# A diffusion-transformer layer: fillers gathered ahead of the first conditioning sums, fewer between them, and the second group's sums one product later

## The chip, the cores and the metric

The kernel runs on one core of a Trainium2 chip. The metric is the device time of one execution in microseconds (us). A core has TensorE (PE; PEld is its weight load), VectorE (DVE), ScalarE (ACT), GpSimd (POOL) and SyncE (SP, which here only issues DMAs). Each works through its own queue of instructions in order.

## The reference

One layer on 256 latent tokens and 256 context tokens of width 2048, in f32. A conditioning vector `c` (and `c_ctx` for the context) makes shifts, scales and gates; the modulated tokens go through one projection for queries, keys and values; windowed and global attention, an output projection, and a SwiGLU network follow.

```python
def ada_mods(cond, w_ada, b_ada):
    m = jnp.einsum('bd,de->be', jax.nn.silu(cond), w_ada) + b_ada      # (2048) x (2048, 12288)
    return [t[:, None, :] for t in jnp.split(m, 6, axis=-1)]
...
sh1, sc1, g1, sh2, sc2, g2 = ada_mods(c, w_ada[layer], b_ada[layer])
csh1, csc1, ... = ada_mods(c_ctx[None, :], w_ada[layer], b_ada[layer])
qa, ka, va, qb, kb, vb = mixer_qkv(x * (1 + sc1) + sh1, w_in[layer], ...)      # u @ w_in, heads, norms
qac, kac, vac, ... = mixer_qkv(ctx * (1 + csc1) + csh1, w_in[layer], ...)
x = layer_norm(ALPHA * x + g1 * (attention(...) @ w_out[layer]), ...)
x = layer_norm(ALPHA * x + g2 * swiglu(x * (1 + sc2) + sh2, ...), ...)
```

The weights are 281 MB; the first thing needed of them are the columns of `w_ada` that give shift and scale of the first 128 channels.

## The kernel before

**Precision.** Each f32 product is made of three matmuls (lines 292 to 294): both operands are split into a high part (a ScalarE cast, `hi`, `uh`) and the rest (a VectorE subtraction, `lo`, `ul`), and hi x hi, lo x hi and hi x lo are summed in PSUM. "A product" below is such a triple, on a bank `acc` of 128 x 512.

**Groups.** The 2048 channels enter the first projection in five groups of 1, 1, 2, 4 and 8 blocks of 128 (`GROUPS`), so that work can start when the shifts and scales of the first block are there. Group 0 has 16 products (six column blocks of `w_in`; two or four row tiles each), and so has group 1.

**Lead-in.** TensorE first runs fillers: `warm(wps, n)` issues n matmuls of the identity with itself (line 342), whose results nobody reads. It then turns `c` and `c_ctx`, which came as rows (`crow`), into columns by one matmul (line 348); ScalarE applies silu (`cs`). The shifts and scales of a group are sums over 2048 rows of `w_ada`: `flow_columns` loads 1 MB for the shifts and 1 MB for the scales and multiplies by `cs` (line 594, 32 output rows at a time, four side by side). For the first group the loads are cut in quarters of 256 KB (line 514), and `quarters` sums a quarter at a time, with fillers after the first three quarters of each MB. Between the two MB the flips (transposes) of the first block of x and ctx (`xt`, `cxt`, line 698) and of the bias (line 368) are pulled in. After the last sums: two fillers, a ScalarE copy `ada` (line 628), small sums with `sel` (line 633), two VectorE additions to shift and scale, seven more fillers, and the first product.

**Order.** A planner (`Flow`) lists all steps of the first part with an estimated duration and sets the order of each engine's queue by simulating them. `F.pulls` overrides it: a pair (trigger, steps) takes the steps out of their place and emits them right behind the trigger. `lead[P, ...]` are the steps of the second group (P = 128 is its first channel): `"both"` its sums over 2 MB, `"copy"`, `"sums"` and `"adds"` what follows on them, `flip`, `mod` and `rest` the transposes of x and ctx, the modulation and the low part. `made` is the list of products of group 0, and `(made, PULL)` stands for its entry PULL, counted from 0. The planner also has 56 filler steps of one matmul each; those whose number is in `WARMS` are emitted, the others are empty.

**Buffers.** Loads of weights go to six buffers of 1 MB (`raw`, `araw`), besides small loads of group 0. SP issues them in order; an issue waits until its buffer has been read, for the conditioning weights by the sums of line 594.

Of the kernel before, what the change touches and what calls it, by code (L numbers as in the profile page):

```python
# [22 lines left out]
P = 128  # L23
# [21 lines left out]
NB4 = 18  # L45
T2K = 5
WARM = 56
WARMS = (32, 33, 35, 36, 37, 38, 39, 40, 41)
SLACK = 2500
AHEAD = 14  # L50
EARLY_G = 2
# [2 lines left out]
LAG_S = 2  # L54
PUT, GET, PLACE = 6, 8, 9
TAIL = 3
PULL = 11
SEED_G = 4
LANDING = 4500, 2500

# [157 lines left out]
def dit_layer(ctx: ExitStack, tc: tile.TileContext, x, c, cx, c_ctx, w_ada, b_ada, w_in, q_norm_g,  # L218
# [15 lines left out]
    def wk_bank():  # L234
        return wk_ps.tile([P, NB], F32, tag="wk", name="wk")
# [104 lines left out]
    def warm(wps, n):  # L340
        for _ in range(n):
            nc.tensor.matmul(wps, lhsT=ident, rhs=ident, start=True, stop=True)  # L342

    wps = Buf("wk")
    wps.t = wk_bank()[:, :P]
    warm(wps.t, 5)
    cps = wk_bank()
    nc.tensor.transpose(cps[:, : 2 * KD], crow, ident[: 2 * KD, : 2 * KD])
    cs = main.tile([P, 72 * 4], F32, tag="cs", name="cs")
# [3 lines left out]
        cps[:, : 2 * KD].rearrange("p (s k) -> p s k", s=2),  # L353
        AF.Silu,
    )


    sel = main.tile([P, 4], F32, tag="sel", name="sel")
# [100 lines left out]
    def const_tables():  # L459
        nc.gpsimd.tensor_scalar_mul(nsink, sinkb, -1.0)  # L460
        for t in range(NT):
            for g, cg, sg in ((gq, cosQ, sinQ), (gk, cosK, sinK)):
# [18 lines left out]
    F = Flow({"raw": RAW_BUFS, "araw": ADA_BUFS, "hl": HL_BUFS, "acc": 4, "wk": 4, "b4": NB4, "t2k": T2K},  # L481
             {"SP": 2100.0, "PE": 3800.0, "ACT": 4300.0, "DVE": 4000.0, "POOL": 4000.0})
# [6 lines left out]
    def t2k(name, shape=(P, NB), dtype=F32):  # L489
        return pa.tile(list(shape), dtype, tag="t2k", name=name, bufs=T2K)  # L490
# [11 lines left out]
    def flow_load(w, k0, nk, c0, width, where=("raw", "araw"), cut=1, small=False):  # L502
        room = Buf(*where)

        def fn():
            if small:
                room.t = b4([P, 2 * NB], F32, "raw1")[:, : nk * width]
                nc.sync.dma_start(room.t, w[k0 * P : (k0 + 1) * P, c0 : c0 + width])
                return
            if cut > 1:  # L510
                room.t = pools[room.pool].tile([P, G4 * NB], F32, tag="raw", name="raw")
                for q in range(0, nk, nk // cut):
                    n = nk // cut
                    nc.sync.dma_start(
                        room.t[:, q * width : (q + n) * width].rearrange("p (k n) -> p k n", k=n),
                        w[(k0 + q) * P : (k0 + q + n) * P, c0 : c0 + width].rearrange("(k p) n -> p k n", p=P),
                    )
                return
            room.t = pools[room.pool].tile([P, G4 * NB], F32, tag="raw", name="raw")[:, : nk * width]
            nc.sync.dma_start(  # L520
                room.t.rearrange("p (k n) -> p k n", k=nk),
                w[k0 * P : (k0 + nk) * P, c0 : c0 + width].rearrange("(k p) n -> p k n", p=P),
            )

        return room, F.add("SP", dma_ns(nk * width * P * 4, width * 4), fn, take=[room])
# [52 lines left out]
    last_load, lead = [], {}  # L578

    def flow_columns(c0, ncol, shift, scale, ats, at):  # L580

        width = ncol * P
        n1 = ncol == 1
        nk = G4 * NB // width
        ns = KD // nk
        bank, prev = Buf("wk"), None

        def fn(g, i, raw, k0, k1):
            if g == i == k0 == 0:
                bank.t = wk_bank()  # L590
            for c in range(k0, k1):
                k = g * nk + c
                j = k % 4
                nc.tensor.matmul(  # L594
                    bank.t[32 * j : 32 * j + 32, :width], lhsT=cs[:, 4 * k + 2 - 2 * i : 4 * k + 34 - 2 * i],
                    rhs=raw.t[:, c * width : (c + 1) * width],
                    start=(i == 0 and k < 4), stop=(i == 1 and k >= KD - 4),
                )

        for g in range(ns):  # L600
            F.at = ats[g]
            (r0, l0), (r1, l1) = (flow_load(w_ada, g * nk, nk, c0 + i * D, width, cut=1 if c0 else 4) for i in range(2))
            last_load[:] = [l1]
            ns1 = nk / 4 * (40 + 1.67 * width)
            if c0:
                def both(g=g, r0=r0, r1=r1):
                    fn(g, 0, r0, 0, nk)
                    fn(g, 1, r1, 0, nk)

                prev = F.add("PE", 2 * ns1 + 420, both, [l0, l1, prev], [bank] if g == 0 else [], [r0, r1])  # L610
            else:
                def quarters(i, r):
                    for q in range(4):
                        fn(0, i, r, 4 * q, 4 * q + 4)
                        if q < 3:
                            warm(wps.t, 1 + i)

                prev = F.add("PE", ns1, lambda r=r0: quarters(0, r), [l0, prev], [bank] if g == 0 else [], [r0])
                lead["sum"] = prev
                prev = F.add("PE", ns1, lambda r=r1: quarters(1, r), [l1, prev], [], [r1])  # L620
            if g == 0:
                lead[c0, "both"] = prev
        F.at = at
        sb, ps = Buf("t2k"), Buf("wk")

        def copy():
            sb.t = t2k("ada")
            nc.scalar.copy(sb.t[:, :width], bank.t[:, :width])

        def sums():  # L630
            ps.t = wk_bank()
            for j in range(ncol):
                nc.tensor.matmul(ps.t[:, 4 * j : 4 * j + 4], lhsT=sb.t[:, j * P : (j + 1) * P], rhs=sel, start=True, stop=True)

        def add(i):
            pv = ps.t[:, 0 : 4 * ncol].rearrange("p (j i s) -> p j i s", i=2, s=2)
            bs, bc = (bcol[:, k : k + ncol, None].to_broadcast([P, ncol, 2]) for k in (c0 // P, c0 // P + KD))
            if i == 0:
                nc.vector.tensor_tensor(shift, pv[:, :, 0, :], bs, op=ALU.add)
            else:  # L640
                nc.vector.scalar_tensor_tensor(scale, pv[:, :, 1, :], 1.0, bc, op0=ALU.add, op1=ALU.add)

        a = F.add("ACT", 60 + 0.9 * width, copy, [prev], [sb], [bank])
        b = F.add("PE", 224 * ncol, sums, [a], [ps], [sb])
        adds = [F.add("DVE", 160, lambda i=i: add(i), [b], give=[ps]) for i in range(2)]
        if n1:
            lead[c0, "copy"], lead[c0, "sums"], lead[c0, "adds"] = a, b, adds
        return a, adds
# [586 lines left out]
    def warm_step(i):  # L1235
        if i in WARMS:
            warm(wps.t, 1)
# [175 lines left out]
    made = lead["products", 0]  # L1413
    F.pulls.append(((lead["products", 1], 3), [lead[2 * P, "both"]]))
    F.pulls.append(((made, PULL), [lead[P, "both"]]))
    F.pulls.append(((made, PULL + 1), [lead[P, "copy"]]))
    F.pulls.append(((made, PULL + 2), [lead[P, "sums"], *lead[P, "adds"], flip0, flip1]))
    F.pulls.append(((made, PULL + 3), [mod0, rest0, mod1, rest1]))
    zroom = [Buf("wk"), Buf("wk")]
    for i in range(2):  # L1420
        F.add("PE", 210, lambda i=i: z_flip(0, 2 * i), [a], [zroom[i]])
# [361 lines left out]
```

## Time and profile before

| | |
|---|---|
| median of 3 runs | 1137.32 us (1136.08 to 1137.8) |
| profiled execution | 1140.03 us, span of its instructions 1138.2 us |
| TensorE busy | 1117.6 us (98%), matmul records 5265 |
| VectorE / ScalarE / GpSimd busy | 842.2 / 548.0 / 40.0 us |
| DMA | 321.26 MB, mean 282 GB/s |
| first product starts | 17.95 us into the span |

Times in the views count from the span's start. A row of the timeline groups equal instructions that follow on each other; "x8" counts records. What stands in brackets is idle time of that engine ahead of the row and who ended it. Matmuls overlap: a row's duration reaches beyond the start of the next, so the pace is read from start to start.

### The profile page before, as it was taken

The page shows a single profiled execution, that of the slowest core. Times are in us where ns is not written, and L with a number is a line of the kernel's source. Part 1 is how long each engine was busy: PE and PEld are TensorE (multiplying, and loading weights), DVE is VectorE, ACT ScalarE, POOL GpSimd, SP SyncE. Part 2 cuts the span into 40 slices and gives each one's busy share as a digit, 9 for nine tenths or more (in the row PEclk, how much of TensorE's full clock was granted, in tenths as well). Part 3 has the DMA queues.
Part 4 walks back from the last instruction along what each step waited for, and adds up shares of the span by engine and source line. Part 5 has one row for each costly group of instructions (what it writes and reads, how often), then busy time and mean ns, then how long its engine had stood idle before and what let it go on. Part 6 is the DMA issues. An engine that isn't in the chain of part 4 may idle for free.

```text
span 1138.2 us, 14088 instructions
## 1 busy us (share of the span) xinstructions
PE 1117.6 (98%) x5265; PEld 896.3 (79%) x5265; DVE 842.2 (74%) x1066; ACT 548.0 (48%) x790; POOL 40.0 (4%) x82
## 2 busy tenths in 40 slices
PE   8999999999999999999999999999999999999996
PEld 6666678788887787888888888888888888888884
DVE  4754579899989988787767566766766788676576
ACT  2322454777874455545464444454544334333342
POOL 1000050110100001000000000000000000000000
PEclk9999999999999999999999999999999999999998
DMA  9999999776999689999867777777687988887541
GB/s 307 324 381 392 389 372 371 271 220 222 360 326 397 212 311 345 324 317 309 321 214 241 228 238 237 219 245 255 216 266 240 313 313 319 315 290 252 194 148 74
DMA packets 178317, 321.26 MB, mean 282 GB/s; under 512 B 8732, under 2 KB 43196, under 8 KB 175943
## 3 DMA queue, kind: packets, MB, share of 16 engines
q1 hardware_dynamic: 177528, 320.03, 81.0%
q8 instruction: 41, 0.67, 0.2%
q10 hardware_dynamic: 720, 0.33, 0.1%
q14 instruction: 28, 0.23, 0.1%
HBM read 304.07 MB, written 16.25 MB: 281 GB/s over the span
## 4 chain that ended last, share of the span: by engine, by line
PE 89%; DVE 4%; DMA 3%; ACT 2%; issue 1%; POOL 0%; SPq 0%; DVEq 0%; ACTq 0%; POOLq 0%
PE acc L292 27%; PE acc L294 27%; PE acc L293 27%; PE wk L594 2%; PE wk L1024 2%; DMA raw<-in_w_in_dram 1%; DMA pd<-hx 1%; DVE lo L545 1%; DVE lo L283 1%; DVE adav L415 1%; DMA raw<-in_w_up_dram 1%; PE wk L292 1%; PE wk L294 1%; PE wk L293 1%; PE wk L342 1%
## 5 line engine op out<-in xcount | busy, mean ns | idle before, releaser
L283 DVE TENSOR_TENSOR lo<-raw,hi 128x1024 fp32r<-128x1024 f32 x258 | 311.8, 1221 | 172.1 <-ACT hi L282 167.6
L282 ACT CAST hi<-raw 128x1024 fp32r<-128x1024 f32 x258 | 270.7, 1055 | 333.7 <-PE acc L294 288.3
L293 PE MATMUL acc<-lo,u2h 128*128 128x512 f32 x704 | 274.0, 389 | 0.8 <-DVE lo L283 0.8
L292 PE MATMUL acc<-hi,u2h 128*128 128x512 f32 x704 | 274.7, 390 | 0.0
L294 PE MATMUL acc<-hi,u2l 128*128 128x512 f32 x704 | 274.1, 389 | 0.0
L293 PEld LDWEIGHTS acc<-lo,u2h 128*128 128x128 f32 x704 | 132.2, 188 | 28.5 <-DVE lo L283 1.1
L292 PEld LDWEIGHTS acc<-hi,u2h 128*128 128x128 f32 x704 | 132.1, 188 | 28.2 <-ACT u2h L1558 0.8
L294 PEld LDWEIGHTS acc<-hi,u2l 128*128 128x128 f32 x704 | 132.1, 188 | 27.8 <-DVE u2l L1559 0.5
L542 ACT CAST hi<-raw 128x1024 fp32r<-128x1024 f32 (+1 forms) x86 | 87.7, 1031 | 108.3 <-DMA raw<-in_w_in_dram 51.5
L292 PE MATMUL acc<-hi,hTh 128*128 128x512 f32 x344 | 135.6, 394 | 0.4 <-ACT acc L1708 0.4
L294 PE MATMUL acc<-hi,hTl 128*128 128x512 f32 x344 | 133.9, 389 | 0.0
L293 PE MATMUL acc<-lo,hTh 128*128 128x512 f32 x344 | 133.9, 389 | 0.0
L415 DVE SCALAR_TENSOR_TENSOR adav<-raw,cs,adav 128x512 f32<-128x512 f32 (+1 forms) x128 | 121.3, 947 | 11.6 <-DMA raw<-in_w_ada_dram 9.4
L545 DVE TENSOR_TENSOR lo<-raw,hi 128x1024 fp32r<-128x1024 f32 (+1 forms) x86 | 101.7, 1193 | 19.0 <-ACT hi L542 18.8
L292 PE MATMUL acc<-hi,uh 128*128 128x512 f32 x256 | 103.0, 402 | 2.4 <-DVE kvacc L781 1.0
L293 PE MATMUL acc<-lo,uh 128*128 128x512 f32 x256 | 100.2, 391 | 1.7 <-DVE lo L545 1.7
L294 PE MATMUL acc<-hi,ul 128*128 128x512 f32 x256 | 100.1, 391 | 0.0
L292 PEld LDWEIGHTS acc<-hi,hTh 128*128 128x128 f32 x344 | 64.6, 188 | 15.1 <-issue 1.0
L293 PEld LDWEIGHTS acc<-lo,hTh 128*128 128x128 f32 x344 | 64.6, 188 | 14.1 <-issue 1.0
L294 PEld LDWEIGHTS acc<-hi,hTl 128*128 128x128 f32 x344 | 64.6, 188 | 13.5
L292 PEld LDWEIGHTS acc<-hi,uh 128*128 128x128 f32 x256 | 48.1, 188 | 20.1 <-issue 6.4
L293 PEld LDWEIGHTS acc<-lo,uh 128*128 128x128 f32 x256 | 48.1, 188 | 11.8 <-DVE lo L545 2.7
(219 smaller groups left out, 1148.8 us busy)
## 6 DMA issues: line engine op xcount, KB each, us to landing
raw<-in_w_ada_dram SPq DMA_DIRECT2D x70, 1024.0 KB, 7.6
raw<-in_w_gate_dram SPq DMA_DIRECT2D x44, 1024.0 KB, 5.3
raw<-in_w_up_dram SPq DMA_DIRECT2D x44, 1024.0 KB, 5.2
raw<-in_w_down_dram SPq DMA_DIRECT2D x44, 1024.0 KB, 4.9
raw<-in_w_ada_dram SPq DMA_DIRECT2D x48, 512.0 KB, 5.5
raw<-in_w_in_dram SPq DMA_DIRECT2D x18, 1024.0 KB, 6.9
raw<-in_w_out_dram SPq DMA_DIRECT2D x16, 1024.0 KB, 8.5
pd<-hx SPq DMA_DIRECT2D x64, 128.0 KB, 4.0
```

Of the source, the lines that this page charges most:

```text
L282: nc.scalar.copy(hi[:, :n], raw[:, s : s + n])
L283: nc.vector.tensor_tensor(lo[:, :n], raw[:, s : s + n], hi[:, :n].bitcast(F32), op=ALU.subtract)
L292: nc.tensor.matmul(ps, lhsT=xh, rhs=w[0], start=first, stop=False, skip_group_check=seeded)
L293: nc.tensor.matmul(ps, lhsT=xh, rhs=w[1], start=False, stop=False, skip_group_check=seeded)
L294: nc.tensor.matmul(ps, lhsT=xl, rhs=w[0], start=False, stop=last, skip_group_check=seeded)
L342: nc.tensor.matmul(wps, lhsT=ident, rhs=ident, start=True, stop=True)
L415: nc.vector.scalar_tensor_tensor(a[:, c : c + piece], raw[:, f : f + piece], cs[:, 4 * (g * (G4 * NB // w) + j) + 2, None], a[:, c : c + p ...
L542: nc.scalar.copy(hl.hi[:, :n], raw.t[:, s : s + n])
L545: nc.vector.tensor_tensor(hl.lo[:, :n], raw.t[:, s : s + n], hl.hi[:, :n].bitcast(F32), op=ALU.subtract)
L594: nc.tensor.matmul(bank.t[32 * j : 32 * j + 32, :width], lhsT=cs[:, 4 * k + 2 - 2 * i : 4 * k + 34 - 2 * i], rhs=raw.t[:, c * width : (c + ...
L1024: nc.tensor.matmul(o_ps.t[:, : 2 * P].rearrange("p (g q) -> p g q", q=32), lhsT=v, rhs=pv[:, k], start=k == 0, stop=k == 3)
```

## The change

Three places. The fillers ahead of the first sums become twelve, seven before the flip of `c` and five after it; those within the first MB go, and within the second there is one each after its second and third quarter (two each after the first three, before). Of the planner's fillers six are emitted instead of nine. And `PULL` goes from 11 to 12, with the pulled steps of the second group regrouped.

```diff
-WARMS = (32, 33, 35, 36, 37, 38, 39, 40, 41)
+WARMS = (32, 33, 35, 36, 37, 38)
...
-PULL = 11
+PULL = 12
...
-    warm(wps.t, 5)
+    warm(wps.t, 7)
     cps = wk_bank()
     nc.tensor.transpose(cps[:, : 2 * KD], crow, ident[: 2 * KD, : 2 * KD])
...
         AF.Silu,
     )
+    warm(wps.t, 5)
...
                         fn(0, i, r, 4 * q, 4 * q + 4)
-                        if q < 3:
-                            warm(wps.t, 1 + i)
+                        if i and 0 < q < 3:
+                            warm(wps.t, 1)
...
     F.pulls.append(((made, PULL), [lead[P, "both"]]))
-    F.pulls.append(((made, PULL + 1), [lead[P, "copy"]]))
-    F.pulls.append(((made, PULL + 2), [lead[P, "sums"], *lead[P, "adds"], flip0, flip1]))
-    F.pulls.append(((made, PULL + 3), [mod0, rest0, mod1, rest1]))
+    F.pulls.append(((made, PULL), [lead[P, "copy"]]))
+    F.pulls.append(((made, PULL + 1), [lead[P, "sums"], *lead[P, "adds"]]))
+    F.pulls.append(((made, PULL + 2), [flip0, flip1, mod0, rest0, mod1, rest1]))
```

The order of VectorE, ScalarE, GpSimd and SP stays as it was; only TensorE's changes. (From line 349 on, lines of the changed kernel are one higher.) TensorE's queue from its start, before: fillers, the flip of `c`, and the first MB with its fillers.

```order
L342 MATMUL wk<-ident 128x128 x5
L348 MATMUL wk<-ident,crow 128x32
L594 MATMUL wk<-raw,cs 32x128 x4
L342 MATMUL wk<-ident 128x128
L594 MATMUL wk<-raw,cs 32x128 x4
...
L698 MATMUL wk<-ident,xt 128x128 x2
```

TensorE's queue from its start in the changed kernel, up to the flips.

```order
L342 MATMUL wk<-ident 128x128 x7
L348 MATMUL wk<-ident,crow 128x32
L342 MATMUL wk<-ident 128x128 x5
L595 MATMUL wk<-raw,cs 32x128 x16
L699 MATMUL wk<-ident,xt 128x128 x2
```

The first MB's 16 matmuls stand in one run behind twelve fillers. Next, TensorE's queue before from the last flip to the first product: the second MB, the small sums (`sel`) and the planner's fillers.

```order
L368 MATMUL acc<-ident,brow 128x96
L594 MATMUL wk<-raw,cs 32x128 x4
L342 MATMUL wk<-ident 128x128 x2
...
L633 MATMUL wk<-sel,ada 128x4
L342 MATMUL wk<-ident 128x128 x7
L292 MATMUL acc<-hi,uh 128x512
```

The same piece of TensorE's queue in the changed kernel.

```order
L369 MATMUL acc<-ident,brow 128x96
L595 MATMUL wk<-raw,cs 32x128 x8
L342 MATMUL wk<-ident 128x128
L595 MATMUL wk<-raw,cs 32x128 x4
L342 MATMUL wk<-ident 128x128
L595 MATMUL wk<-raw,cs 32x128 x4
L342 MATMUL wk<-ident 128x128 x2
L634 MATMUL wk<-sel,ada 128x4
L342 MATMUL wk<-ident 128x128 x4
L292 MATMUL acc<-hi,uh 128x512
```

Seven fillers are gone from this piece. Last, TensorE's queue before around the second group's sums (the x32 row), which stand behind the twelfth product.

```order
L594 MATMUL wk<-raw,cs 32x128 x32
L292 MATMUL acc<-hi,uh 128x512
L293 MATMUL acc<-lo,uh 128x512
L294 MATMUL acc<-hi,ul 128x512
...
L633 MATMUL wk<-sel,ada 128x4
L698 MATMUL wk<-ident,xt 128x128 x2
L698 MATMUL wk<-ident,cxt 128x128 x2
```

The same piece of TensorE's queue in the changed kernel, behind the thirteenth product.

```order
L595 MATMUL wk<-raw,cs 32x128 x32
L292 MATMUL acc<-hi,uh 128x512
L293 MATMUL acc<-lo,uh 128x512
L294 MATMUL acc<-hi,ul 128x512
L634 MATMUL wk<-sel,ada 128x4
...
L699 MATMUL wk<-ident,xt 128x128 x2
L699 MATMUL wk<-ident,cxt 128x128 x2
```

Between the sums and the small sums stood two products and now stands one; the flips stood right behind the small sums and now follow after one more product.

## Prediction, made before the changed kernel had run

> **What bounds the kernel now.** I read the page first, its busy row and the chain that ended last, then TensorE's timeline of the first 45 us.
>
> ```profile
> PE 1117.6 (98%) x5265; PEld 896.3 (79%) x5265; DVE 842.2 (74%) x1066; ACT 548.0 (48%) x790; POOL 40.0 (4%) x82
> ...
> PE 89%; DVE 4%; DMA 3%; ACT 2%; issue 1%; POOL 0%; SPq 0%; DVEq 0%; ACTq 0%; POOLq 0%
> ```
>
> TensorE is busy 98% of the span and makes 89% of the chain, so whatever brings its stream forward for good reaches the end. The change touches only the first 35 us; the columns are start, duration, instruction, records (an f32 matmul leaves two, a transpose one), idle before.
>
> ```profile
> 1.46 2.50 PE L342 MATMUL wk<-ident 128*128 128x128 f32 x10 [1.46 <-POOL ident masks.py:199]
> 4.50 0.28 PE L348 MATMUL wk<-ident,crow 32*128 32x32 f32 x1 [0.53 <-DMA crow<-in_c_ctx_dram]
> 5.10 0.65 PE L594 MATMUL wk<-raw,cs 128*32 128x128 f32 x8 [0.32 <-ACT cs L351]
> 5.68 0.80 PE L342 MATMUL wk<-ident 128*128 128x128 f32 x2
> 6.41 0.66 PE L594 MATMUL wk<-raw,cs 128*32 128x128 f32 x8
> ...
> 9.62 0.69 PE L698 MATMUL wk<-ident,xt 128*128 128x128 f32 x2
> ...
> 10.83 0.66 PE L594 MATMUL wk<-raw,cs 128*32 128x128 f32 x8
> ...
> 13.15 1.23 PE L342 MATMUL wk<-ident 128*128 128x128 f32 x4
> 14.31 0.45 PE L594 MATMUL wk<-raw,cs 128*32 128x128 f32 x8
> 14.69 0.71 PE L342 MATMUL wk<-ident 128*128 128x128 f32 x4
> 15.33 0.43 PE L594 MATMUL wk<-raw,cs 128*32 128x128 f32 x8
> 15.69 0.71 PE L342 MATMUL wk<-ident 128*128 128x128 f32 x4
> ...
> 16.38 1.81 PE L342 MATMUL wk<-ident 128*128 128x128 f32 x14
> 17.95 0.47 PE L292 MATMUL acc<-hi,uh 128*128 128x512 f32 x1
> ...
> 44.58 0.49 PE L292 MATMUL acc<-hi,uh 128*128 128x512 f32 x1 [0.50 <-ACT hi L542]
> ```
>
> Two fillers (L342) take 1.16 us from 13.15 to 14.31, but 0.64 from 14.69 to 15.33; a quarter MB of sums (L594) takes 0.58 at 5.10 and 0.36 at 15.33. So TensorE ran at about half speed until about 14.4 us. From 5.10 on it never waits for a landing: at half speed it is itself the bound. The quarters come sooner, by the DMA issues of the first and second MB:
>
> ```profile
> L514 SPq DMA_DIRECT2D raw<-in_w_ada_dram x2: 368/406/444, 3.5 to 3.9; - x2
> DMA to landing us min/median/max: 4.7/4.7/4.7
> ...
> L514 SPq DMA_DIRECT2D raw<-in_w_ada_dram x1: 734/734/734, 6.6 to 6.6; - x1
> ```
>
> The one issued at 3.5 us lands 4.7 later, at 8.2; it is the fourth of eight (the eighth is issued at 6.6). If the eighth takes as long it lands at 11.3, and those between, by an estimate from these two, every 0.78 us: 9.0, 9.8, 10.5. The sums of the eighth began at 15.33, 4 us after that.
>
> What restores full speed? Stretches of the clock column, with length, busy times of PE, PEld, DVE, ACT and POOL, granted clock, DMA share, GB/s; and one eight-record group on either side:
>
> ```profile
> 348.90:352.30 3.40, 1.38 (x6) 0.85 (x5) 3.40 (x4) 1.91 (x2) 0.00 (x0) 1.00 1.06 355
> 352.30:355.70 3.40, 3.40 (x9) 2.68 (x8) 3.37 (x5) 1.16 (x3) 0.00 (x0) 0.51 1.01 368
> ...
> 344.92 1.89 PE L1024 MATMUL wk<-pT,kvacc 128*128 128x256 f32 x8
> ...
> 352.74 3.38 PE L1024 MATMUL wk<-pT,kvacc 128*128 128x256 f32 x8
> ```
>
> After 3.4 us in which TensorE was busy 1.38, it ran at 0.51 for 3.4 us, and at full speed again after that busy stretch; the same eight records took 3.38 instead of 1.89. So the clock is judged over stretches of about 3.4 us. The column has no entry for the slow start (it reads 1.00 there); the durations show it. The Trainium skill ("TensorE: Matmul & The Clock Gate", Part 1) describes such a gate: half rate by default, full after a busy window of about 3.4 us, the windows running freely.
>
> **The change, part by part.**
>
> 1. Fillers. Seven instead of five stand before the flip of c, and five follow it. One costs 1.16 - 0.73 = 0.43 us at the margin (two: 13.15 to 14.31; one alone between sums: 5.68 to 6.41, of which 0.30 is the switch). Seven from 1.46 reach 4.5 to 4.8, where the flip began at 4.50: 0 to 0.3 us late, I take 0.2. Flip 0.3, then 5 x 0.43 + 0.3: the first sums start at about 7.2 instead of 5.10, 2.1 us late. What fills the wait is the point: TensorE is solid from 1.46 on. Before, no 3.4 us stretch ahead of 11 us was solid: 2.50 us of fillers and then idle up to 4.50; after that sums, switches and flips; full speed came only after 10.83 to 14.31, two fillers to each quarter. A solid stretch of 5.5 us holds a window of 3.4 wherever it starts, or nearly all of one: I take full speed from about 7 us; 1.46 plus one window, 4.9, would be early and 1.46 plus two, 8.3, the latest.
>
> 2. First MB in one run: three fillers go, at 0.73 each (half speed). Three quarters are there at 7.2 and take 3 x 0.36; the fourth waits for 8.2 and ends at 8.55. The flips of x, ctx and the bias took 1.21 (9.62 to 10.83), at full speed 0.6: 9.15.
>
> 3. Second MB: fillers fall from two after each quarter to one, only after its second and third. The quarters now wait for landings: the one of 9.0 is past, 9.8, 10.5, then 11.3 + 0.36 = 11.7, against 15.33 + 0.36 = 15.69. That is 4.0 us earlier; a filler (0.32, half of 0.64) fits the gap of 0.4 that each landing leaves behind the sums.
>
> 4. Four fillers instead of seven ahead of the first product cost nothing either way. The chain there, with start and length:
>
> ```profile
> 16.82 0.57 ACT uh L709
> ...
> 17.42 0.55 DVE uf L711
> ...
> 17.97 0.61 DVE lo L545
> ...
> 18.62 0.49 PE acc L293
> ...
> 28.39 0.23 PE acc L294
> 28.62 1.88 PE wk L594 x64
> ...
> 37.44 5.97 DMA raw<-in_w_in_dram
> ```
>
> The second matmul of the first product waited until 18.62 for VectorE, not for fillers. This chain of ScalarE and VectorE follows the sums, and moves 4.0 earlier whole.
>
> 5. The second group's first sums come one product later: three matmuls of 0.23, 0.69 us. They end at 28.62 + 1.88 = 30.50 now, and would at 30.5 - 4.0 + 0.7 = 27.2. Their small sums follow after one product instead of two, but the flips after two as before, so inputs of group 1 stand at the same distance; between 0 and one product (0.69) could be lost where its first products start, I take 0.2, since its copy still has a product to hide in.
>
> 6. What hangs on these sums is the weight stream:
>
> ```profile
> 30.56 0.34 SPq L520 DMA_DIRECT2D raw<-in_w_in_dram  x1
> ...
> SPq L520 <- PE wk L594: 10.6, 2, 8.6
> ...
> 28.00:32.00 4.00, 4.00 (x75) 3.18 (x74) 0.69 (x1) 1.92 (x4) 0.00 (x0) 1.00 0.16 25
> 32.00:36.00 4.00, 3.74 (x20) 2.85 (x19) 3.59 (x9) 2.56 (x5) 0.00 (x0) 1.00 0.81 250
> ...
> 48.00:52.00 4.00, 4.00 (x23) 3.42 (x22) 3.85 (x8) 1.65 (x3) 0.00 (x0) 1.00 1.05 403
> ```
>
> SP's queue stood 8.6 us until L594 freed a buffer, and issued at 30.56; the DMAs moved 25 GB/s in 28 to 32 and 250 in 32 to 36. The stage after waits for that stream: the chain's DMA of 37.44 to 43.41, a cast, then TensorE at 44.58 after an idle of 0.50. Issued 3.3 earlier, at 27.3, the stream follows on the one that ends at about 28, and the hole closes. In 28 to 36 it moved 1.1 MB; at the 403 GB/s of 48 to 52 it would have moved 3.2, so 5.2 us were lost there. The stream can thus come forward by 3.3 to 5.2, and TensorE, itself 3.1 to 3.3 ahead, gains beyond that at most the waits at this place, of which the 0.50 at 44.58 is the one shown. From 48 on TensorE is full (4.00 of 4.00) and nothing there gives the gain back.
>
> Sum: -4.0 + 0.7 + 0.2 = -3.1, and -0.5 for the wait at 44 us: -3.6. On the profiled execution's own time (span 1138.2, 1140.03 with what lies around it) that gives 1136.4. The median is 1137.32, 2.7 below the profiled one; I carry the difference over to it: 1133.7.
>
> **Rivals.**
>
> A. The clock opens early and closes again. From 8 to 11.5 us TensorE waits for landings between short sums; I count 0.36 x 5 + 0.6 + 0.64 = 3.0 of 3.4 us busy, but with switches inside. The row above shows a halving after 1.38 of 3.40. If it closes, the products from 14.6 on run at half speed for up to 3.4 us, which costs 1.7; 3.6 less that leaves 1.9, or 1.3 with the slow sums ahead: 1135.7. [...] Against the rival: 3.0 of 3.4 is far above 1.38.
>
> B. It does not open early, because the fillers' density was not what it wanted. Then the first sums run from 7.2 at half speed, 4 x 0.58 to 9.5, flips to 10.7, four quarters 2.3 and two fillers at 0.73 to 14.5: 1.2 earlier than 15.69, less 0.7 for the later sums: -0.5, 1136.8.
>
> C. Slower. As in B, but with fillers thinned out (six to two in the second MB, seven to four) the clock also opens one or two windows later than 14.4. Products at half speed cost 1.7 us per window: with B's -0.5 this is +1.2 for one and +2.9 for two: 1138.5 to 1140.2. It decides when TensorE is still slow at 21 us. Against it: the solid 5.5 us at the start.
>
> D. It does nothing: the landings after 28 us set the pace whatever TensorE does. Then the hole in the stream would have to stay though its buffer is freed 3.3 us sooner; the row SPq <- PE wk L594 names the sums as what held it. 1137.3.
>
> **How the numbers follow.** The forecast has 0.68, A 0.14, B 0.11, C 0.05, D 0.02. The forecast's own range is -2.5 to -5.3: the gain is larger where the old kernel opens its clock a window later than in the profile (another second of fillers and slow sums), and 1 us smaller where it opens sooner. So 1132.0 to 1134.8 (1137.3 less these); with A and B 1132.0 to 1136.6. 0.2%, about what a measurement here can tell from no change, is 2.3 us, 1135.05. Faster: all of the forecast but 0.02, and a third of A, 0.70; same: the rest of A and of the forecast, B, D and a little of C, 0.25; slower: most of C, 0.05.
>
> **What the profile after would show.** Right: two fillers in about 0.45 to 0.65 us and flips in 0.6 before 10 us; sums of the last quarter starting near 11.3, right behind its landing; the first product near 14; the sums of the second group ending near 27; no row of 25 GB/s around 30; TensorE's first product of the next stage near 41. Wrong: fillers still 0.43 each after 8 us (B); products of 0.46 a matmul after 14 us (A, C); a start at 41 that turns back into waits before 60 us.

## The result, and the profile after

The changed kernel takes 1134.97 us (median of 20 runs, 1132.26 to 1138.16), the old one beside it 1137.5 (20 runs, 1134.42 to 1140.93). The ratio is 0.9979, with a 95% interval of 0.997 to 0.9988: 2.4 us faster, between 1.4 and 3.4. The forecast was 1133.7, within 1132.0 to 1136.6. The profiled execution took 1134.76 us, its span 1133.0.

TensorE's timeline of the changed kernel, the lead-in first, then the places after it that the prediction named (start, duration, instruction, records, idle before):

```profile
1.46 3.36 PE L342 MATMUL wk<-ident 128*128 128x128 f32 x14 [1.46 <-POOL ident masks.py:199]
...
4.99 1.71 PE L342 MATMUL wk<-ident 128*128 128x128 f32 x10
6.62 0.86 PE L595 MATMUL wk<-raw,cs 128*32 128x128 f32 x24
8.11 0.42 PE L595 MATMUL wk<-raw,cs 128*32 128x128 f32 x8 [0.63 <-DMA raw<-in_w_ada_dram]
8.47 0.44 PE L699 MATMUL wk<-ident,xt 128*128 128x128 f32 x2
...
9.14 0.88 PE L595 MATMUL wk<-raw,cs 128*32 128x128 f32 x16
9.95 0.49 PE L342 MATMUL wk<-ident 128*128 128x128 f32 x2
10.41 0.43 PE L595 MATMUL wk<-raw,cs 128*32 128x128 f32 x8
...
11.18 0.42 PE L595 MATMUL wk<-raw,cs 128*32 128x128 f32 x8
...
13.29 0.50 PE L292 MATMUL acc<-hi,uh 128*128 128x512 f32 x1
14.47 0.51 PE L293 MATMUL acc<-lo,uh 128*128 128x512 f32 x1 [0.67 <-DVE lo L546]
...
25.08 1.95 PE L595 MATMUL wk<-raw,cs 128*32 128x128 f32 x64
...
30.75 0.50 PE L294 MATMUL acc<-hi,ul 128*128 128x512 f32 x1 [0.31 <-DVE ul L727]
...
36.36 0.47 PE L292 MATMUL acc<-hi,uh 128*128 128x512 f32 x1 [0.57 <-DVE kvacc L780]
...
41.16 0.51 PE L292 MATMUL acc<-hi,uh 128*128 128x512 f32 x1
42.24 0.50 PE L293 MATMUL acc<-lo,uh 128*128 128x512 f32 x1 [0.58 <-DVE lo L546]
...
48.99 1.92 PE L595 MATMUL wk<-raw,cs 128*32 128x512 f32 x16
```

The five fillers from 4.99 take 1.63 to the next start, 0.33 each. That lies between the half speed of 0.43 and the full speed of 0.22 (the old kernel's seven from 16.38 to 17.95), so the clock opened while they ran. The same five take 1.31 to the next start where the clock is open from their first (4.80 to 6.11 in the run with the order undone, below). Here they take 0.32 more, which is about one and a half of them at half speed; by this estimate the clock opened at about 5.6 us. From 6.62 the sums run at full speed, overtake the data and wait for the landing at 8.11: the lead-in is now set by the DMAs. A filler and its way back to the sums take 0.46 (9.95 to 10.41) and 0.42 (10.76 to 11.18) instead of 0.73. The last sums start at 11.18 instead of 15.33, and the second matmul of the first product at 14.47 instead of 18.62.

The same kernel's SP timeline (the issue behind the second group's sums), and then stretches of the clock column (length, busy times of PE, PEld, DVE, ACT, POOL, granted clock, DMA share, GB/s):

```profile
27.09 0.34 SPq L521 DMA_DIRECT2D raw<-in_w_in_dram  x1
```

```profile
28.00:32.00 4.00, 3.64 (x17) 2.29 (x16) 3.06 (x8) 1.87 (x4) 0.00 (x0) 1.00 0.98 327
...
44.00:48.00 4.00, 4.00 (x23) 3.43 (x22) 3.91 (x8) 1.88 (x4) 0.00 (x0) 1.00 1.06 411
```

SP issues at 27.09 instead of 30.56. The hole in the weight stream, 25 GB/s in 28 to 32, is filled with 327. (In the two later profiles of the old kernel the hole is shallower, 116 and 129 GB/s; the two later ones of the changed kernel have 273 and 285.) In 44 to 48, where TensorE waited in the old kernel, it is busy 4.00 of 4.00. That is later work, though: what stood behind the waits now runs from 41.16, and it still waits once, 0.58 at 42.24. Of the old kernel, two rows of TensorE's timeline and that stretch:

```profile
45.84 0.50 PE L293 MATMUL acc<-lo,uh 128*128 128x512 f32 x1 [0.77 <-DVE lo L545]
...
52.58 1.92 PE L594 MATMUL wk<-raw,cs 128*32 128x512 f32 x16
```

```profile
44.00:48.00 4.00, 2.73 (x14) 1.99 (x11) 3.13 (x5) 2.47 (x4) 0.00 (x0) 1.00 1.05 408
```

The row at 52.58 is TensorE's first block of sums for the third group. It is the last common mark of the early stages, and at 48.99 the changed kernel is 3.6 us ahead there. The row at 45.84 follows the one at 44.58 that the prediction shows: the old kernel waits here twice, 0.50 and 0.77. The two spans differ by 5.2. Of this, 1.5 is the half-speed stretch at 352.30 that the prediction showed of the old kernel (3.38 against 1.89 for the same records), which this execution of the changed kernel doesn't have.

### The profile page after: what moved, and what is told of

It reads as the page before. It is cut to its first block, busy times and chain, and to the rows that moved or that the text cites. A ratio compares the mean times of both kernels' runs of the same rounds, so it can differ in the third digit from the quotient of the medians.

```text
span 1133.0 us, 14075 instructions
## 1 busy us (share of the span) xinstructions
PE 1111.8 (98%) x5259; PEld 892.6 (79%) x5259; DVE 841.2 (74%) x1066; ACT 547.5 (48%) x790; POOL 39.7 (4%) x82
## 4 chain that ended last, share of the span: by engine, by line
PE 91%; DMA 4%; DVE 2%; ACT 2%; issue 0%; POOL 0%; DVEq 0%; SPq 0%; ACTq 0%; POOLq 0%
PE acc L292 28%; PE acc L294 27%; PE acc L293 27%; PE wk L1025 2%; PE wk L595 2%; DMA raw<-in_w_in_dram 2%; DMA raw<-in_w_ada_dram 1%; DMA pd<-hx 1%; DVE lo L546 1%; PE wk L292 1%; PE wk L294 1%; PE wk L293 1%; DMA raw<-in_w_gate_dram 1%; DVE lo L283 1%; ACT hi L543 0%
```

## The experiments

The theory: the solid fillers open TensorE's clock early, so that the first sums go at the pace of the landings; that, and nothing else in the change, brings the gain, and the later order gives a part of it back. Against it stand the prediction's rivals, and one more: that the gain comes of the fillers taken away, or of the order. Kernels of one comparison share the runs of the old kernel.

**The twelve fillers alone.** The old kernel with

```diff
-    warm(wps.t, 5)
+    warm(wps.t, 7)
...
+    warm(wps.t, 5)      # behind the silu
```

> The old kernel with one part of the change: seven fillers ahead of the flip of c and five behind it. Theory (the solid run of fillers opens TensorE's clock early): fillers take 0.22 us each before 8.5 us instead of after 14.4; the kept fillers in the second MB (0.64 + 0.36 a quarter at full speed, more than the 0.78 between landings) put the last sums at about 12.5 instead of 11.5 in the changed kernel and 15.7 in the old one; with the second group's sums not delayed, -2.3 to -3.3 us against the old kernel, about 1134.7. Rival (what costs time are the fillers between the quarters, not the clock): the first sums only start 1.5 to 2 us later and the rest follows, 0 to +2 us, 1137.5 to 1139.5.

Measured: 1135.0 us (12 runs), ratio 0.9983 (0.9971 to 0.9995). Rows of this kernel's timeline, TensorE and SP:

```profile
6.96 0.49 PE L342 MATMUL wk<-ident 128*128 128x128 f32 x2
...
12.95 0.43 PE L595 MATMUL wk<-raw,cs 128*32 128x128 f32 x8
...
28.19 0.34 SPq L521 DMA_DIRECT2D raw<-in_w_in_dram  x1
```

A filler between sums takes 0.42 from its start to the next (6.96 to 7.38, the next row of sums) where the old kernel's took 0.73: the clock is open. With all the old fillers between the quarters the last sums start at 12.95, 1.8 later than in the changed kernel, and yet the gain is 1.9 us (0.0017 of 1137.8) of the 2.4 that the whole change brings. So the fillers alone carry the sign of the result. Their third group's sums start at 48.65, about where the changed kernel's do (48.99 here, 48.22 and 48.13 in two later profiles): what the thinning adds, the later order takes away again, as the runs below show.

**Fewer fillers alone.** The old kernel with

```diff
-WARMS = (32, 33, 35, 36, 37, 38, 39, 40, 41)
+WARMS = (32, 33, 35, 36, 37, 38)
...
-                        if q < 3:
-                            warm(wps.t, 1 + i)
+                        if i and 0 < q < 3:
+                            warm(wps.t, 1)
```

> The old kernel with the other part of the lead-in alone: no fillers in the first MB, one after the second and third quarter of the second MB, six planner's fillers instead of nine; five fillers ahead of the flip as before, none behind it. Theory (clock): the clock opens no earlier than in the old kernel; at half speed the last sums end at about 13.7 (2 us earlier), but the clock opens at 14 to 18 or later, so products start at half speed and 1.7 us go again for each 3.4 us of it: -1 to +1.5 us, 1136.5 to 1139. Rival (the fillers between are the cost): most of the gain, -2.5 to -3.5, about 1134.5.

Measured: 1137.96 us (12 runs), ratio 1.0006 (0.9993 to 1.0018). Rows of this kernel's timeline, TensorE and SP:

```profile
13.21 0.66 PE L594 MATMUL wk<-raw,cs 128*32 128x128 f32 x8
...
15.10 2.05 PE L342 MATMUL wk<-ident 128*128 128x128 f32 x8
...
29.49 0.34 SPq L520 DMA_DIRECT2D raw<-in_w_in_dram  x1
```

The sums come 2.1 us earlier than in the old profile, at half speed (0.66 a group instead of 0.43); but four fillers behind them take 1.70 us to the first product (15.10 to 16.80), 0.43 each, where the changed kernel takes 1.05 for four (12.24 to 13.29): the clock is still closed at 15 us, and whatever follows until it opens is slow. SP issues at 29.49, 1.1 sooner than in the first old profile and no sooner than in the two below, and no time is gained. Thinning the fillers is worth something only once the clock is open.

**The order alone.** The old kernel with

```diff
-PULL = 11
+PULL = 12
...
-    F.pulls.append(((made, PULL + 1), [lead[P, "copy"]]))
-    F.pulls.append(((made, PULL + 2), [lead[P, "sums"], *lead[P, "adds"], flip0, flip1]))
-    F.pulls.append(((made, PULL + 3), [mod0, rest0, mod1, rest1]))
+    F.pulls.append(((made, PULL), [lead[P, "copy"]]))
+    F.pulls.append(((made, PULL + 1), [lead[P, "sums"], *lead[P, "adds"]]))
+    F.pulls.append(((made, PULL + 2), [flip0, flip1, mod0, rest0, mod1, rest1]))
```

> The old kernel with only the second group's sums one product later and its steps regrouped. Theory: SP's next issue is 0.7 us later (31.2 instead of 30.5), the hole in the DMA stream grows, 0 to +0.7 us: 1137.5 to 1138.2. Rival (this order is part of the gain): -0.5 to -1 us, 1136.7. Its profile is also a second look at when the old lead-in opens the clock: the theory of free-running windows expects some moment between 11 and 18 us, not 14.4 again.

Measured: 1138.97 us (12 runs), ratio 1.0008 (0.9995 to 1.0021). Rows of this kernel's timeline, TensorE and SP:

```profile
15.18 0.42 PE L594 MATMUL wk<-raw,cs 128*32 128x128 f32 x8
...
31.11 0.34 SPq L520 DMA_DIRECT2D raw<-in_w_in_dram  x1
...
34.77 0.50 PE L294 MATMUL acc<-hi,ul 128*128 128x512 f32 x1 [0.31 <-DVE ul L726]
```

Its last sums start at 15.18, as in the old profile (15.33), and SP issues 0.55 later (31.11 against 30.56), or 0.70 counted from the last sums, which is one product. TensorE has a wait of 0.31 for the low part `ul` of the second group. The profiles of the old kernel and of the two kernels with the change's lead-in and `PULL` 11 don't have it. The median is higher; the interval doesn't exclude no change.

**The order undone.** The changed kernel with the three old pulls, so with the fillers of the change alone:

```diff
-PULL = 12
+PULL = 11
...
-    F.pulls.append(((made, PULL), [lead[P, "copy"]]))
-    F.pulls.append(((made, PULL + 1), [lead[P, "sums"], *lead[P, "adds"]]))
+    F.pulls.append(((made, PULL + 1), [lead[P, "copy"]]))
+    F.pulls.append(((made, PULL + 2), [lead[P, "sums"], *lead[P, "adds"], flip0, flip1]))
...
```

> The changed kernel with the second group's sums back behind the twelfth product, everything else as changed. Theory: SP's next issue comes 0.7 us earlier than in the changed kernel (26.4 instead of 27.1), but the running transfer only ends near 28 (31.97 landed in the changed kernel), so at most a part of it arrives: 0 to -0.7 us against the changed kernel, 1134.3 to 1135.0. Rival (the later place is needed, since its loads land late): +0.5 to +1 us, 1135.5 to 1136. The clock opens before 8.5 us here too.

Measured: 1133.87 us (12 runs), ratio 0.9972 (0.9959 to 0.9985). Rows of this kernel's timeline, TensorE and SP:

```profile
4.80 1.38 PE L342 MATMUL wk<-ident 128*128 128x128 f32 x10
...
11.26 0.42 PE L595 MATMUL wk<-raw,cs 128*32 128x128 f32 x8
...
26.47 0.34 SPq L521 DMA_DIRECT2D raw<-in_w_in_dram  x1
...
46.88 1.92 PE L595 MATMUL wk<-raw,cs 128*32 128x512 f32 x16
```

The lead-in is that of the changed kernel (11.26, 11.18). SP issues at 26.47, 0.62 sooner than in the first profile of the changed kernel, and the third group's sums start 2.1 sooner than there. Neither wait that the changed kernel has at 36 and 42 us is here, and none of those that the old kernel has at 44.

**Seven ahead, none behind the flip.** The changed kernel with

```diff
-    warm(wps.t, 5)      # behind the silu; the seven ahead of the flip stay
```

> The changed kernel without the five fillers behind the flip of c; seven stand ahead of it. Theory (the clock wants a stretch of about 3.4 us of nearly solid work): the solid run is 3.0 us and is followed by waits for landings, so in most executions the clock opens only with the fillers and products after 11 us; at half speed the last sums end near 13.7 as with thinning alone, and products start slow: +1 to +3.5 us against the changed kernel, 1136 to 1138.5. Rival (seven are enough, five only delay the sums): the clock opens before 6 us, the sums are bound by landings either way, the same time as the changed kernel, 1135.

Measured: 1137.79 us (12 runs), ratio 0.9996 (0.9982 to 1.001). Rows of this kernel's timeline, TensorE and SP:

```profile
13.01 0.66 PE L594 MATMUL wk<-raw,cs 128*32 128x128 f32 x8
13.59 0.71 PE L342 MATMUL wk<-ident 128*128 128x128 f32 x4
...
29.17 0.34 SPq L520 DMA_DIRECT2D raw<-in_w_in_dram  x1
```

The seven fillers end at about 4.8, and the gap behind the flip while ScalarE works (0.32) is back. All eight quarters then run at half speed; the clock opens at 13.5, between the sums of 0.66 and the two fillers of 0.71. The whole gain is gone: without the five behind the flip the change brings nothing over its 12 runs. What the five do is not the same in every execution. In four of the seven profiles of kernels with all twelve, the clock opened while the seven still ran: their row is 3.16 to 3.29 us long, not 3.36, and the five behind them take 1.38, full speed from the first. In the other three it opened among the five. Whether the five then open the clock or keep it open, these runs don't tell apart.

**The changed and the old kernel once more,** as they are, in the same comparison.

> The changed kernel once more, for a second look at its lead-in and for more executions. Theory: the clock opens between 4.4 and 8.3 us at some other moment than 5.7, the last sums start behind their landing at about 11.2 all the same, SP issues the next weights at about 27.1; -2 to -3.6 us against the old kernel. Rival (the clock sometimes closes again or opens late, which is why the gain measured is 2.5 and not 3.6): a lead-in at half speed somewhere between 6 and 18 us.

> The old kernel once more. Theory (windows run freely): its clock opens at another moment than 14.4, between 11 and 18 us, so its own time spreads by 1 to 2 us from this alone; ratio to the old kernel 1.000 within 0.0012. Rival (the moment is fixed by the program): 14.4 again.

Measured: the changed kernel 1135.32 us (11 runs), ratio 0.9977 (0.9966 to 0.9987); the old one 1137.93 (12 runs), ratio 0.9995 (0.998 to 1.0009). Two rows of the changed kernel's timeline come first, then some of the old one's, with two stretches of its clock column:

```profile
11.33 0.43 PE L595 MATMUL wk<-raw,cs 128*32 128x128 f32 x8
...
27.24 0.34 SPq L521 DMA_DIRECT2D raw<-in_w_in_dram  x1
```

```profile
11.41 0.71 PE L342 MATMUL wk<-ident 128*128 128x128 f32 x4
...
14.05 0.43 PE L594 MATMUL wk<-raw,cs 128*32 128x128 f32 x8
...
29.30 0.34 SPq L520 DMA_DIRECT2D raw<-in_w_in_dram  x1
...
43.63 0.49 PE L292 MATMUL acc<-hi,uh 128*128 128x512 f32 x1 [0.81 <-ACT hi L542]
...
44.90 0.50 PE L293 MATMUL acc<-lo,uh 128*128 128x512 f32 x1 [0.77 <-DVE lo L545]
```

```profile
42.10:45.50 3.40, 1.82 (x20) 0.85 (x12) 1.57 (x2) 1.94 (x3) 0.00 (x0) 1.00 1.05 405
45.50:48.90 3.40, 3.40 (x10) 2.63 (x9) 2.77 (x4) 1.04 (x1) 0.00 (x0) 0.50 1.05 409
```

The old lead-in isn't always the one that was profiled first. Here two fillers at 11.41 have a row of 0.71, as those at 14.69 had in the first profile: the clock opened near 11.4, not 14.4, and the last sums start 1.3 us earlier. The old kernel also lost its clock at 45.50, right behind two waits at 44 us, the first of which is the one that the prediction counted on removing. Its third group's sums start at 53.22, where the old kernel's third profile, whose last sums start within 0.02 us of these and whose clock stays open here, has 51.41.

**No fillers behind the twelve.** The changed kernel with

```diff
-WARMS = (32, 33, 35, 36, 37, 38)
+WARMS = ()
...
-                        if i and 0 < q < 3:
-                            warm(wps.t, 1)
```

> The changed kernel with all fillers behind the first MB taken out (two in the second MB, two and four around the small sums); the twelve ahead stay. Theory: full speed once won is kept as long as a window is more than about 41% busy; from 8 to 14 us TensorE has some 3.5 us of sums, flips and small sums in 6, so one window may fall under it: the clock closes in some executions, and products start slow: 0 to +2 us against the changed kernel, 1135 to 1137. Rival (only an idle window closes it): it stays open, first product as early as in the changed kernel, 1135.

Measured: 1136.72 us (12 runs), ratio 0.9983 (0.9971 to 0.9995). Rows of the timeline, and two stretches of the clock column:

```profile
15.90 0.63 PE L292 MATMUL acc<-hi,uh 128*128 128x512 f32 x1
16.33 0.63 PE L293 MATMUL acc<-lo,uh 128*128 128x512 f32 x1
...
18.23 0.40 PE L292 MATMUL acc<-hi,uh 128*128 128x512 f32 x1
18.47 0.40 PE L293 MATMUL acc<-lo,uh 128*128 128x512 f32 x1
...
28.79 0.34 SPq L521 DMA_DIRECT2D raw<-in_w_in_dram  x1
```

```profile
11.10:14.50 3.40, 1.51 (x19) 0.64 (x11) 1.04 (x4) 1.80 (x4) 0.00 (x0) 1.00 0.94 318
14.50:17.90 3.40, 3.02 (x7) 2.48 (x8) 3.05 (x6) 1.53 (x2) 0.00 (x0) 0.51 1.06 320
```

This is rival A, seen: TensorE is busy 1.51 of the 3.40 us up to 14.50, and then runs at 0.51 for 3.40; a matmul of a product follows the one ahead after 0.43 instead of 0.24. SP issues 1.55 later than in the changed kernel beside it (28.79 against 27.24). Of this 0.26 was there before the clock closed: the second matmul of the first product starts at 14.88 against 14.62. So the closing cost about 1.3. The fillers taken out, two among the sums, two ahead of the small sums and the four ahead of the first product, which the prediction's step 4 costed at nothing, are what keeps TensorE busy here: the same stretch of the changed kernel beside it is busy 2.84 of 3.40, and in its three profiles no stretch of 3.4 us between 4.5 and 21 us is busy less than 2.36, wherever it begins. That the clock closes without them is seen in one profile. On the whole time this is less sharp: the medians are 1.4 apart (1136.72 against 1135.32), but the intervals overlap.

**Last, old, order undone and changed once more,** in one comparison.

> The old kernel a third time, for a further look at its lead-in. So far its clock opened at 14.4, 13.5 and 11.35 us, and SP issued the weights behind the second group's sums at 30.56, 31.11 (with the later order) and 29.30. Theory: again a moment between 11 and 15 us, the issue 29 to 31 us accordingly; ratio 1.000 within 0.0012. Rival: the early 11.35 was a single case and it opens at 14 or later.

> The changed kernel with the second group's sums back behind the twelfth product, again, now beside the changed kernel in one call. Theory: 0.7 us earlier at SP's issue (26.5 against 27.1 to 27.2) and no wait of 0.31 for the low part of group 1's inputs; 0.5 to 1 us faster than the changed kernel, -3 to -3.6 against the old one. Rival: the two cannot be told apart and the first comparison was chance.

> The changed kernel a third time, beside the run with the order undone. Theory: clock open before 8.3 us, issue at 27.1 to 27.3, -2 to -3.4 us against the old kernel, 0.5 to 1 us slower than with the order undone. Rival: no difference to it.

| | median, us (runs) | ratio (95%) | last sums start | SP issues |
|---|---|---|---|---|
| old | 1137.5 (12) | 0.9998 (0.9983 to 1.0012) | 14.03 | 29.22 |
| changed, order undone | 1133.3 (6) | 0.9955 (0.9939 to 0.9971) | 11.62 | 26.80 |
| changed | 1135.93 (12) | 0.9978 (0.9964 to 0.9992) | 11.50 | 27.37 |

TensorE's start of the third group's sums, of the old kernel, of the one with the order undone, and of the changed one:

```profile
51.41 1.92 PE L594 MATMUL wk<-raw,cs 128*32 128x512 f32 x16
```

```profile
47.21 1.92 PE L595 MATMUL wk<-raw,cs 128*32 128x512 f32 x16
```

```profile
48.13 1.92 PE L595 MATMUL wk<-raw,cs 128*32 128x512 f32 x16
```

The kernel with the order undone has the lowest median in both of its comparisons, though its interval overlaps its neighbour's each time (0.9972 beside 0.9983 for the fillers alone, 0.9955 beside 0.9978 for the changed kernel, with only 6 runs in the latter case). It beats the old one by 3.2 to 5.1 us (0.0028 and 0.0045 of 1137.5), where the changed one gains 2.4 to 2.6.

## Why the prediction was right, and where its sum was off

**The clock (step 1)** was right, its number late: it was to open at about 7 us, and did so at about 5.6 here, and before 4.8 with the order undone (the five from 4.80 run in 1.38 us, which is full speed from the first). The latter is before the 4.9 that the prediction called early, and after no more than 3.3 us of fillers, a little less than a whole stretch of 3.4. The sums started at 6.62, not 7.2, since the clock opened among the fillers themselves. (The 7.2 also leaves out the 0.2 by which the flip was taken to be late.) With seven alone the profiled execution stayed at half speed and the gain was gone, although in other executions the seven had opened the clock by themselves.

**The lead-in (steps 2 to 4)** came out as worked out: the landing at 8.11 against 8.2 taken, the flips in 0.67 (8.47 to 9.14) against 0.6, the last sums at 11.18 against 11.3, a filler and its switch in 0.42 to 0.46 where 0.32 was taken. Two things add up here, as two runs apart show: the open clock with all the old fillers brings the last sums to 12.95, and the fillers taken out bring the rest of the way to 11.18; the second without the first gained no time. The theory's "nothing else" is too strong in this: the fillers taken out add to the gain, once the clock is open. At the third group's sums, with the old order, they are worth 1.6 (48.65 with the fillers alone, 46.88 and 47.21 with them taken out too); on the time 1.1 in the comparison that has both, with overlapping intervals.

**The later sums (step 5)** were mis-sized by little. They were to come 0.69 later, and SP issues 0.6 later (27.09, 27.24 and 27.37 against 26.47 and 26.80, by their means). The 0.2 for group 1's inputs is the wait of 0.31 for `ul`. At the third group's sums the difference is larger, about 1.4 (48.99, 48.22 and 48.13 in the three profiles of the changed kernel, mean 48.45; 46.88 and 47.21 with the order undone, mean 47.05), since the changed kernel sometimes has waits that the other doesn't show: 0.57 at 36 and 0.58 at 42 us in the first profile, 0.26 at 41 in the second, none in the third. So 1.4 rather than 0.9.

**The stream (step 6)** closed its hole as forecast. The second group's sums ended near 27.0 (27.2 forecast), and TensorE's first product behind the next sums started at 41.16 (near 41 forecast). The wait of 0.50 that was to go did go. It was sized too small, though: the old kernel waits at this place twice, for the high part and one matmul later for VectorE's low part, 0.50 and 0.77, 0.81 and 0.77, 0.67 and 0.77 in its three profiles. The changed kernel's three have no wait for the high part, and 0.58, 0.26 and none for the low part. In the mean the waits here fell by 1.15 (1.43 to 0.28), where the sum had 0.5.

**The terms that were off.** The largest is step 3's 4.0. It measured the new lead-in against one execution of the old one, whose clock opened at 14.4. Four profiles with the old lead-in (three of the old kernel, one with the order alone) start the last sums at 15.33, 15.18, 14.05 and 14.03, mean 14.65; five with the new one at 11.18, 11.33, 11.50, 11.26 and 11.62, mean 11.38. The typical gain in these profiles is 3.3, not 4.0. SP's issue, which has the later order in it, tells the same: 30.56, 29.30 and 29.22 in the old kernel's profiles, mean 29.69; 27.09, 27.24 and 27.37 in the changed one's, mean 27.23; 2.46 between them, where 3.3 was forecast. The order cost 1.4 instead of 0.9, and the waits at 44 us were worth more than the 0.5 of the sum. With the first two alone the forecast's -3.6 would become -2.4, about what the timed runs gave; but that leaves out the third, and it is not shown that the 2.4 comes about in this way. A weak step of the forecast is the one from the profile to the median: the profiled old execution was 2.7 slower than the median of the first three runs, and this was carried over unchanged, although its late clock is a part of that excess which the change takes away (its last sums start 1.3 later than in the two later profiles). The prediction had allowed for a clock that opens sooner (1 us less) and, on the other side, for one that opens a window later, which no profile showed; with one profile to go by it could have leant to the smaller side. (B's own 1136.8 lies outside the 1136.6 that is given as the end of the range with A and B.)

**The rivals.** A is a real mechanism, at a price a little under the one that was given (1.7 forecast, about 1.3 at SP's issue); none of the changed kernel's three profiles has it in the lead-in. B is what the profiled execution with seven fillers does. C's later opening was not seen in the changed kernel; the kernel with fewer fillers alone, still at half speed at 15 us, is its nearest relative. D is excluded by the stream, which moved with the sums: SP's issue and the 25 GB/s in 28 to 32.

**What stays open.** At the third group's sums the means of the profiles are 3.95 apart (52.58, 53.22 and 51.41 for the old kernel, mean 52.40), and the profiled times themselves (1140.03, 1138.92 and 1138.23; 1134.76, 1137.45 and 1132.98) 4.0 on average, while the timed runs give 2.4. The timed runs of each of the two kernels scatter with a standard deviation of 1.7 us, so the difference of two means of three has one of 1.4 (1.7 times the root of 2/3), and 4.0 and 2.4 can't be told apart. In these six executions nothing is given back later: from the third group's sums to the end of the span the old kernel takes 1085.6, 1083.9 and 1085.0 us, mean 1084.8, and the changed one 1084.0, 1087.5 and 1083.1, mean 1084.9. The three old executions that were profiled are slow ones for their kernel (mean 1139.1, median of its timed runs 1137.5), the changed ones are not. Why they are slow, beyond the late clock of the first and the closed one of the second, stays open; so does how often a lead-in opens its clock late, since only profiles show it, and these come from executions on different chips.

## What to carry to other kernels

Where a kernel begins with short matmuls that wait for data, put one unbroken run of full-size fillers ahead of them, long enough to fill a window of the clock wherever it falls, and keep a few thin ones up to the first long stretch of work: seven ahead (3.3 us) gained nothing here, twelve (5.2 us) did, with the clock open before the first sums in all seven profiles that have them, and with no fillers behind the twelve the clock closed again in the execution that was profiled. Don't judge a start-up by one profile, since the phase in which the clock opens differs from execution to execution: price the gain against several, and lean to the mean. And test the parts of a change apart; here one of the three, the later order, by all that the profiles show cost time.

## What was not expected of the hardware

TensorE's clock can close after a window in which it is busy, but not enough: 1.51 of 3.40 us at 11.10 in the kernel without later fillers, 1.82 of 3.40 at 42.10 in the old one. The Trainium skill ("TensorE: Matmul & The Clock Gate", Part 1, the table of the two states) has it close after at least one idle window; these rows and the one at 348.90 of the prediction are busy for 1.38 to 1.82 us, and they decide. The same half-speed window also came near 350 us in the second profile of the changed kernel, behind a window that was busy 1.39 of 3.40:

```profile
345.90:349.30 3.40, 1.39 (x7) 0.82 (x6) 3.40 (x5) 1.77 (x2) 0.00 (x0) 1.00 0.90 284
349.30:352.70 3.40, 3.40 (x10) 2.64 (x9) 3.37 (x5) 1.30 (x3) 0.00 (x0) 0.50 1.05 376
```

It is the same place as in the old kernel's first profile, and 1.5 us or so of the scatter between executions. The clock closed there in three of the thirteen profiles, these two and the one with seven fillers. In these three the one wait of TensorE ahead of it, for VectorE, is 2.02, 2.01 and 2.17 us long; in the others it is at most 1.82 or absent.

And sums with 32 output rows, with transposes and single fillers between, were slow to open the clock, though TensorE waited for nothing: the old kernel ran them at half speed from 5.10 on. In its first profile the clock opened only at 14.4 us, behind two pairs of fillers; in the two later ones it opened at 11.4, behind this mixture alone. What of it the clock does not count was not taken apart.
